# Three edits to a hybrid decoder block: router logits on two halves of the array, fewer idle products, shared squares and a split store at the end

## The chip, the cores and the metric

The kernel runs on one core of one Trainium2 chip. The time is device microseconds of one execution, the median over several; the kernel before took 1893.37 us (three runs, 1891.93 to 1896.53). The engines are PE (TensorE; PEld are its weight loads), DVE (VectorE), ACT (ScalarE), POOL (GpSimd) and SP, whose queue issues nearly all DMA.

## The reference

One decoder layer over 512 tokens of width 2048, in float32: a modulated RMSNorm, a combined input projection, sliding-window attention (16 heads) beside forgetting attention (16 heads), an output projection, and then a hierarchical mixture of experts. The parts that matter here are the router and the end:

```python
x   = x + g_a * (mixed @ w_out[l])
h2  = rmsnorm(x, norm_moe_g[l]) * (1.0 + sc_m) + sh_m

g_logits = (t @ w_group) + b_group            # 4 groups, top 1
e_logits = ((t @ w_expert) + b_expert).reshape(N, N_GROUPS, EXPERTS_PER_GROUP)
e_in = take_along_axis(e_logits, g_sel)       # the 8 experts of that group
top_val, top_idx = lax.top_k(e_in, 2)
...                                           # 2 of 32 SwiGLU experts per token, width 512
x = x + g_m * moe
return rmsnorm(x, final_g)                    # (1, 512, 2048)
```

## The kernel before, in words

The order of the work on every engine is written out by hand: each engine executes its instructions in the order in which the program issues them, and waits on semaphores for its inputs. The 512 tokens are four blocks (tb = 0 to 3) of 128, on the partitions; the width is four chunks (cc) of 512 columns.

**Out-projection and logits.** The output projection runs chunk by chunk (2, 0, 1, 3). For each chunk, products named oq (lines L214 to L216, three for each pair of a high and a low part) accumulate in PSUM; DVE multiplies by the gate and adds to x (gx at L1108, x at L1109). A `Tail` object then takes the chunk's blocks one by one, in steps between the next chunk's products: `tr` transposes x (x1T, copied to x1Ts by ACT at L1127) and squares it, and `logit` forms the chunk's share of the router's 36 logits (4 groups and 32 experts): four products at L1132 with x1Ts as weights and 36 columns of the scaled router weights `wrf` as moving operand. DVE puts the first chunk's share into `lg` (L1134) and adds the next two (L1136). The last chunk's shares stay in one PSUM tile, `lp4`, and are added at L1199, after the row norms `rs` are there. In the same stretch, the modulation vectors of the expert part are formed from w_ada: pieces of 512 KB go through the tile `raw` (which the pieces of w_out share), DVE accumulates half of each (L621), ACT scales the other half (L623) and POOL accumulates it (L624, the first by L619). ACT and DVE also split each piece of w_out into a high and a low part (L175, L176).

**Choosing the experts.** DVE scales the logits by `rs` (L1211), adds the bias (L1212) and runs a row of small steps to the chosen group and experts (`chosen_b`, L1253). PE meanwhile runs 22 products of the identity with itself whose results nobody reads (`turn`, L1229), then the ranking products `rk` (L1257), then 8 more. DVE makes slots and one-hot rows from the ranks (L1468). ACT (L1480) and DVE (L1486) split x times `rs` into two parts, and PE gathers the tokens of each expert with the one-hot rows (xe, L1499); ACT and DVE move the result to SBUF (L1508, L1506).

**Experts.** The 32 experts go in 16 pairs, two experts side by side on the halves of the array (64 columns each): pg and pu (L1363), y (L1385), and the return to token order o (L1407). SP loads the weights, 1 MB a tile, into a ring of tiles, each as soon as the tile's former content has been used (L1309).

**The end.** The last pair's down projection goes in five pieces of columns, `CHUNKS` (three of 512, two of 256): y (L1423), the return to token order (L1442), DVE's addition to x (L1446). After each block of each piece `last_norm` has ACT square the sum and add up the squares (L1605, into `sf5`). After the last, DVE adds up the five sums (L1608), scales them (L1609) and forms the inverse root with ACT's root (L130 to L134); then come eight pieces of 128 by 1024, scaled by DVE (L1616) and stored by SP (L1617). A loop for experts with over 64 tokens follows, which runs no round with these inputs.

Of the kernel before, what the change touches and what calls it, by code (L numbers as in the profile page):

```python
# [8 lines left out]
F32 = mybir.dt.float32  # L9
# [3 lines left out]
AF = mybir.ActivationFunctionType  # L13
OP = mybir.AluOpType
AX = mybir.AxisListType

T = 512
D = 2048
TB = 4
EPS = 1e-6  # L20
# [33 lines left out]
def kernel(  # L54
# [8 lines left out]
    V, S, G, PE, SP = nc.vector, nc.scalar, nc.gpsimd, nc.tensor, nc.sync  # L63
# [8 lines left out]
    def bcast(v, n):  # L72
        return bass.AP(tensor=v.tensor, offset=v.offset, ap=[[0, 128], [1, n]])
# [5 lines left out]
    def flat(t):  # L79
        return t.rearrange("p a b -> p (a b)")  # L80
# [18 lines left out]
    ident = big.tile([128, 128], F32, name="ident")  # L99
# [28 lines left out]
    def rsqrt_(dst, v, tmp):  # L128

        S.activation(tmp, v, AF.Sqrt)  # L130
        V.reciprocal(dst, tmp)
        V.scalar_tensor_tensor(tmp, dst, -0.5, dst, op0=OP.mult, op1=OP.mult)
        V.tensor_mul(tmp, tmp, v)
        V.scalar_tensor_tensor(dst, tmp, 1.5, dst, op0=OP.add, op1=OP.mult)  # L134
# [373 lines left out]
    def bank(shape, name):  # L508

        return pb["pool"].tile(shape, F32, tag=pb["tag"], name=name, bufs=pb["bufs"])  # L510
# [328 lines left out]
    def side_step():  # L839
        f = side_late.pop(0) if side_late else None  # L840
        if f:
            f()

    def attend(segs):


        us = [(u, i) for i, sg in enumerate(segs) for u in sg[0]]
        counts = [sum(1 for _, j in us if j == i) for i in range(len(segs))]
        late, at = None, -1
        for k in range(len(us) + LAG):  # L850
            u, i = us[k] if k < len(us) else (None, len(segs) - 1)
            if i != at:
                if at >= 0:
                    fill.drain()
                at = i
                _, make, total, hook = segs[i]
                fill = make()
                step = total / (2.0 * counts[i] + (2.0 * LAG if i == len(segs) - 1 else 0.0))
                if hook:
                    hook(fill)  # L860
                if u.pre:
                    u.pre()
                    fill.take(1.3)
            if u:
                u.a1()
            if 0 < k <= len(us):
                us[k - 1][0].a2()
            fill.take(step)
            if late:
                late()  # L870
                late = None
            if k >= LAG:
                us[k - LAG][0].b()
                late = us[k - LAG][0].c
            fill.take(step)
            if k + 1 < len(us) and us[k + 1][1] == at and us[k + 1][0].pre:
                us[k + 1][0].pre()
            else:
                side_step()
        late()  # L880
        return fill
# [19 lines left out]
    for g in range(4):  # L901
        VP += natural(256, lambda g=g: accs("accv", f"vb{g}"),
                      lambda tb, o, g=g: S.activation(vbs[g][:, tb, :], o, AF.Copy))

    def fills(i):
        for kind, n, *to in FILLS[i]:
            if kind == "v":
                for v in VP[n:to[0]]:
                    yield from v
            else:  # L910
                yield from (queries2 if kind == "q" else heads2)(n)
# [59 lines left out]
    def out_first():  # L971

        rr = mx["rr"]
        for cc in range(3):
            oacc[cc] = accs4(f"op{cc}")
            for n in range(4):
                hi, lo = ws.get()
                if cc == 2 or n < 3:
                    for j in range(2):
                        k = 2 * n + j  # L980
                        if not cc and k + AH < 8:
                            mixed(k + AH, rr)
                        out_kt(oacc[cc], hi, lo, n, j)
                        if not cc and k in (4 - AH, 7 - AH):
                            load_x1(int(k == 7 - AH))
                        yield 2.6
                else:
                    for tb in range(TB):
                        for j in range(2):
                            out_kt(oacc[cc], hi, lo, n, j, (tb,), last=7)  # L990
                        m = spare()
                        V.tensor_mul(m, oacc[cc][tb], gates[0][:, cc * 512:(cc + 1) * 512])
                        G.tensor_add(x1[cc][:, tb, :], x1[cc][:, tb, :], m)
                        yield 1.3

    wrf = wr.rearrange("p c j e -> p (c j) e")
# [27 lines left out]
    def more_o(fill):  # L1024
# [3 lines left out]
    total = lambda i: 2.56 * sum(to[0] - n if to else 8 for _, n, *to in FILLS[i])  # L1028
    last6 = list(fox_units((6,), qks, vbs))
    f = attend([  # L1030
        (swa_units(((0, 2), (1, 3), (4, 6), (5, 7))[i]) if i < 4 else
         fox_units((i - 4,), qks, vbs) if i < 10 else last6[:LAST], lambda i=i: Fill(fills(i), side, RATE), total(i),
         hooks.get(i))
        for i in range(11)
    ] + [(last6[LAST:] + list(fox_units((7,), qks, vbs)), lambda: Fill(out_first()), LAST_FILL, router)])
# [20 lines left out]
    mo = ctx.enter_context(tc.tile_pool(name="mo", bufs=1, reuse_waits="tile"))  # L1056
    gm = mo.tile([128, D], F32, name="gm")
    ss2 = mo.tile([128, TB, 4], F32, name="ss2")
    lg = mo.tile([128, TB, 36], F32, name="lg")

    def sm(shape, name, dt=F32):
        return mo.tile(shape, dt, name=name)

    def bc(t, shape):
        return t.to_broadcast(shape)

    rs = sm([128, TB], "rs")
    ss3 = sm([128, TB], "ss3")
    iota = sm([128, 128], "iota")
# [21 lines left out]
    class Tail:  # L1091
# [35 lines left out]
            S.activation(self.xT[tb], t, AF.Copy)  # L1127

        def logit(self, tb):
            lp = self.lp4[:, tb, :] if self.last else bank([128, 36], f"lp_{self.cc}_{tb}")  # L1130
            for j in range(4):
                PE.matmul(lp, self.xT[tb][:, j, :], wrf[:, self.cc * 4 + j, :], start=j == 0, stop=j == 3)  # L1132
            if self.cc == 2:
                V.tensor_copy(lg[:, tb, :], lp)  # L1134
            elif not self.last:
                V.tensor_add(lg[:, tb, :], lg[:, tb, :], lp)  # L1136

        def steps(self):
            for tb in range(TB):
# [22 lines left out]
    tail = Tail(2, oacc[2])  # L1162
# [3 lines left out]
    for cc, first in ((0, 4), (1, 4), (3, 0)):  # L1166
        steps = chain(steps, tail.steps())
        ops = []
        for i in range(4):
            k = bank6 % 6  # L1170
# [3 lines left out]
        tail = Tail(cc, ops)  # L1174
# [21 lines left out]
    tail.logit(2)  # L1196
    rms_x1()
    tail.logit(3)
    V.tensor_add(lg, lg, tail.lp4)  # L1199
    pst.close()  # L1200
    frt.close()

# [5 lines left out]
    pb["pool"], pb["tag"], pb["bufs"], hold[0] = ps, "y", 4, True  # L1208
    while side_late:
        side_step()  # L1210
    V.tensor_mul(lg, lg, bc(rs[:, :, None], [128, TB, 36]))  # L1211
    V.tensor_add(lg, lg, bc(brt[:, None, :], [128, TB, 36]))  # L1212

    def one_hot(v, n, mx_, name):
# [11 lines left out]
    def turn(n):  # L1226

        for _ in range(n):
            PE.matmul(idle[:, :128], ident, ident, start=True, stop=True)  # L1229

    turn(22)
    gl = lg[:, :, 0:4]
    gmax = sm([128, TB], "gmax")
    V.tensor_reduce(gmax, gl, axis=AX.X, op=OP.max)
# [20 lines left out]
    for tb in range(TB):  # L1255
        for k in range(tb + 1):
            PE.matmul(rk[:, tb, :], before if k == tb else ones_b, chosen_b[:, k].rearrange("p g e -> p (g e)"),  # L1257
                      start=k == 0, stop=k == tb)
    turn(8)
    place = sm([128, TB, 4, 8], "place")  # L1260
    pf = place.rearrange("p t g e -> p t (g e)")
    V.scalar_tensor_tensor(place, chosen_b, FAR, bc(off.rearrange("p a b e -> p (a b) e")[:, None], [128, TB, 4, 8]),
                           op0=OP.mult, op1=OP.add)
# [19 lines left out]
    HID = cw[:, 5120:5632]  # L1283
# [4 lines left out]
    YT = [cw[:, 5632:6144], more_f[:, 1, :], big.tile([128, 512], F32, tag="wr", name="yt2"), HID]  # L1288
# [6 lines left out]
    def ring_tile():  # L1295

        n = nld[0]
        nld[0] += 1
        if 8 <= n < 12 or 20 <= n < 24:
            return rp_.tile([128, 4, 512], F32, tag=f"x2{n % 12 - 8}", name=f"w{n}")  # L1300
        k = n if n < 8 else n - 4 if n < 20 else n - 8
        return (mo, rp_)[k // 4 % 2].tile([128, 4, 512], F32, tag="w", name=f"w{n}", bufs=4)
# [211 lines left out]
    def total(tb):  # L1514

        if not x2s:
            x2s.extend(rp_.tile([128, D], F32, tag=f"x2{i}", name=f"x2_{i}") for i in range(TB))
        return x2s[tb]
# [77 lines left out]
    sf5 = sm([128, TB, 5], "sf5")  # L1596
    sf, rf, tf = sm([128, TB], "sf"), sm([128, TB], "rf"), sm([128, TB], "tf")

    def last_norm(cols, tb=0):
        if cols is None:  # L1600
            SP.dma_start(fg, bcast(final_g, D))
            return
        c0, c1 = cols
        i = CHUNKS.index(cols)
        S.activation(HID[:, :c1 - c0], total(tb)[:, c0:c1], AF.Square, accum_out=sf5[:, tb, i:i + 1])  # L1605
        if c1 < D or tb < 3:
            return
        V.tensor_reduce(sf, sf5, axis=AX.X, op=OP.add)  # L1608
        V.tensor_scalar(sf, sf, 1.0 / D, EPS, op0=OP.mult, op1=OP.add)  # L1609
        rsqrt_(rf, sf, tf)  # L1610
        for tb in range(TB):
            y = ring_tile()
            for h in range(2):
                sl = slice(h * 1024, (h + 1) * 1024)
                yv = flat(y)[:, sl]
                V.scalar_tensor_tensor(yv, total(tb)[:, sl], rf[:, tb:tb + 1], fg[:, sl], op0=OP.mult, op1=OP.mult)  # L1616
                SP.dma_start(out[tb * 128:(tb + 1) * 128, sl], yv)  # L1617
# [113 lines left out]
```

## Time and profile before

| | |
|---|---|
| median of three runs | 1893.37 us |
| the profiled execution: time, span | 1895.8 us, 1893.9 us |
| mean granted TensorE clock | 0.981 |
| busy: PE, PEld, DVE, ACT, POOL | 96%, 60%, 54%, 40%, 15% |
| DMA | 573.84 MB, 303 GB/s on average |
| the chain that ended last | PE 74%, DMA 8%, ACT 7%, DVE 7%, issue 3%, POOL 1% |
| out-projection with the logits | about 764 to 891 us |
| choosing experts to the first expert product | about 891 to 906 us |
| expert pairs | to about 1866 us |
| squares, root, stores | to 1893.9 us |

A row of the timeline reads: start, duration, engine, line, operation, out<-in, shapes, and in brackets the idle time before it and what ended it. "x8" merges eight instructions. Each float32 product appears as two records. A table by stretches gives busy time of the engines in each stretch, then the granted clock, the share of time in which the DMA engines were busy, and GB/s. The chain lists what each step on the way to the end was released by.

### The profile page before, as it was taken

Reading aid. Unit: us, or ns where it says so; the run is one execution under the profiler, and the core shown is the slowest. Engines: PE = TensorE matmul, PEld = TensorE weight load, DVE = VectorE, ACT = ScalarE, POOL = GpSimd, SP = SyncE. Lnnn points to the kernel's source line nnn. Section 1 sums busy time; section 2 is a strip of 40 time slices with the busy share of each in tenths; the row PEclk is TensorE's granted clock in tenths of the full one; section 3 lists DMA queues with packets and bytes.
Section 4 is the critical chain, followed back from the end, with each engine's and each line's share of the span. In section 5 each row is a group of like instructions: output and inputs, shape, how many; then the busy total and the mean of one; then the engine's idle time right before and its main releaser. Section 6 shows DMA issues by size and latency. Waiting matters only on the chain.

```text
span 1893.9 us, 26581 instructions
## 1 busy us (share of the span) xinstructions
PE 1810.1 (96%) x10045; PEld 1131.1 (60%) x10045; DVE 1018.6 (54%) x1812; ACT 748.7 (40%) x1462; POOL 288.2 (15%) x217
## 2 busy tenths in 40 slices
PE   7998999899899999999999999999999999999995
PEld 5668887787787777778544454444444444444432
DVE  4334676666566545757555454544554545545435
ACT  3235656565555443345523233232322323323213
POOL 0000434443354321445000000000000000000000
PEclk8998999999999999999999999999999999999998
DMA  9984555565566342668989999999999999999995
GB/s 338 352 274 106 169 164 152 165 196 173 160 186 186 113 142 78 208 214 295 369 344 397 420 419 421 421 420 420 420 418 421 416 420 420 419 420 416 420 413 215
DMA packets 208791, 573.84 MB, mean 303 GB/s; under 512 B 22624, under 2 KB 110728, under 8 KB 159888
## 3 DMA queue, kind: packets, MB, share of 16 engines
q1 hardware_dynamic: 207744, 572.00, 80.3%
q8 instruction: 81, 1.33, 0.3%
q14 instruction: 54, 0.44, 0.1%
q10 hardware_dynamic: 912, 0.07, 0.0%
HBM read 567.82 MB, written 4.19 MB: 302 GB/s over the span
## 4 chain that ended last, share of the span: by engine, by line
PE 74%; DMA 8%; ACT 7%; DVE 7%; issue 3%; POOL 1%; SPq 0%; DVEq 0%; ACTq 0%; POOLq 0%
PE pu L1363 12%; PE pg L1363 11%; PE y L1385 9%; PE xe L1499 7%; PE o L1407 5%; DMA w<-in_w_up_dram 4%; PE qp L214 3%; PE qp L216 3%; PE qp L215 3%; DMA raw<-in_w_ada_dram 2%; PE gv L325 2%; PE acc L214 1%; PE acc L215 1%; PE acc L216 1%; PE ob L826 1%
## 5 line engine op out<-in xcount | busy, mean ns | idle before, releaser
L1363 PE MATMUL pu<-w,cw 128*64 128x512 f32 x1024 | 239.3, 593 | 4.7 <-DMA w<-in_w_up_dram 4.7
L1363 PE MATMUL pg<-w,cw 128*64 128x512 f32 x1024 | 235.5, 598 | 1.3 <-ACT cw L1508 0.8
L1508 ACT ACTIVATE cw<-xe,shM,scM 128x128 f32<-128x128 f32 x128 | 58.5, 458 | 429.2 <-PE xe L1499 396.2
L1385 PE MATMUL y<-w,more_f 128*64 128x512 f32 x960 | 214.2, 598 | 4.1 <-ACT xp_whi L1480 2.3
L1506 DVE TENSOR_SCALAR cw<-xe,scM,shM 128x128 f32<-128x128 f32 x128 | 52.4, 410 | 299.3 <-ACT cw L1508 299.3
L624 POOL TENSOR_TENSOR gb<-gb,raw 128x512 f32<-128x512 f32 x112 | 162.1, 1448 | 275.8 <-ACT raw L623 211.4
L1410 DVE SCALAR_TENSOR_TENSOR x<-o,wpair,x 128x512 f32<-128x512 f32 x240 | 163.2, 743 | 19.3 <-PE o L1407 19.3
L1363 PEld LDWEIGHTS pu<-w,cw 128*64 128x64 f32 x1024 | 76.0, 137 | 154.1 <-issue 140.3
L1480 ACT ACTIVATE xp_whi<-x,rs 128x256 fp32r<-128x256 f32 x236 | 162.6, 762 | 0.9 <-DVE rs L134 0.9
L1385 PEld LDWEIGHTS y<-w,more_f 128*64 128x64 f32 x960 | 71.2, 137 | 134.4 <-issue 111.1
L1363 PEld LDWEIGHTS pg<-w,cw 128*64 128x64 f32 x1024 | 69.7, 136 | 133.5 <-issue 128.4
L176 DVE TENSOR_TENSOR wlo_s<-raw,whi_s 128x512 fp32r<-128x512 f32 x96 | 91.4, 953 | 107.7 <-ACT whi_s L175 107.6
L1486 DVE SCALAR_TENSOR_TENSOR xp_wlo<-x,rs,xp_whi 128x256 fp32r<-128x256 f32 x232 | 144.8, 681 | 2.2 <-ACT xp_whi L1480 2.2
L621 DVE SCALAR_TENSOR_TENSOR ga<-raw,csil,ga 128x512 f32<-128x512 f32 x112 | 111.3, 994 | 26.2 <-DMA raw<-in_w_ada_dram 25.6
L1499 PE MATMUL xe<-cr,xp_whi 128*128 128x256 f32 x472 | 120.5, 294 | 0.0
L1499 PEld LDWEIGHTS xe<-cr,xp_whi 128*128 128x128 f32 x472 | 88.7, 188 | 47.3 <-issue 45.4
L1499 PE MATMUL xe<-cr,xp_wlo 128*128 128x256 f32 x472 | 114.3, 281 | 0.0
L214 PE MATMUL qp<-hT_hi,whi_s 128*128 128x512 f32 x256 | 107.3, 419 | 0.0
L216 PE MATMUL qp<-hT_hi,wlo_s 128*128 128x512 f32 x256 | 101.2, 395 | 0.0
L215 PE MATMUL qp<-hT_lo,whi_s 128*128 128x512 f32 x256 | 101.2, 395 | 0.0
L623 ACT ACTIVATE raw<-raw,csil 128x512 f32<-128x512 f32 x112 | 79.8, 713 | 34.0 <-DMA raw<-in_w_ada_dram 32.7
L1499 PEld LDWEIGHTS xe<-cr,xp_wlo 128*128 128x128 f32 x472 | 88.9, 188 | 0.0
(445 smaller groups left out, 3372.5 us busy)
## 6 DMA issues: line engine op xcount, KB each, us to landing
w<-in_w_gate_dram SPq DMA_DIRECT2D x128, 1024.0 KB, 10.6
w<-in_w_up_dram SPq DMA_DIRECT2D x128, 1024.0 KB, 13.9
w<-in_w_down_dram SPq DMA_DIRECT2D x126, 1024.0 KB, 10.3
raw<-in_w_ada_dram SPq DMA_DIRECT2D x128, 512.0 KB, 4.2
raws<-in_w_ada_dram SPq DMA_DIRECT2D x64, 512.0 KB, 8.9
raw<-in_w_in_dram SPq DMA_DIRECT2D x160, 128.0 KB, 2.8
raw<-in_w_out_dram SPq DMA_DIRECT2D x32, 512.0 KB, 3.8
raw<-in_w_in_dram SPq DMA_DIRECT2D x48, 256.0 KB, 3.3
```

What stands on the lines that cost most here:

```text
L214: PE.matmul(o, lhi, rhi, start=first, stop=False, **kw)
L215: PE.matmul(o, lhi, rlo, start=False, stop=False, **kw)
L216: PE.matmul(o, llo, rhi, start=False, stop=last, **kw)
L621: V.scalar_tensor_tensor(a, ts[n][:, j, :], s, a, op0=OP.mult, op1=OP.add)
L624: G.tensor_add(a, a, ts[n][:, j, :])
L1363: PE.matmul(o[64 * e:64 * e + 64, :], self.xe(cc)[:, j, 64 * e:64 * e + 64], w[cc, e][:, j, :], start=cc == 0 and j == 0, stop=cc == 3 and ...
L1385: PE.matmul(ys[dc][64 * e:64 * e + 64, :], HT[:, k, 64 * e:64 * e + 64], self.wd[k, e][:, dc, :], start=k == 0, stop=k == 3)
L1407: PE.matmul(o, self.ohT[:, tb, :], v, start=i == 0, stop=i == 1)
L1410: V.scalar_tensor_tensor(x2, o, self.w_col(tb), x2 if self.n else x1[dc][:, tb, :], op0=OP.mult, op1=OP.add)
L1480: S.activation(hi[tb], xv, AF.Identity, scale=s)
L1486: V.scalar_tensor_tensor(lo[tb], xv, s, hi[tb].bitcast(F32), op0=OP.mult, op1=OP.subtract)
L1499: PE.matmul(t[:, j, :], v[tb][:, j, :], OHS[:, tb].rearrange("p q s -> p (q s)"), start=tb + i == 0, stop=tb + i == TB)
```

## The change

Three edits, joined.

*Logits.* For chunks 2, 0 and 1 the roles of the operands are exchanged: the 36 columns of `wrf` are the weights and the transposed x is the moving operand, 128 columns. The four products of a visit go alternately to output partitions 0 to 35 and 64 to 99, that is to two halves of the array's columns. DVE then copies or adds both parts into a new tile `lgT` (partitions by tokens). In the last chunk a product of `lgT` with `both`, two identities stacked at partitions 0 and 64, turns the sum back and adds the halves up in `lp4`, ahead of the four products of the old form. The addition of `lp4` goes: one instruction multiplies `lp4` by `rs` straight into `lg`. POOL clears and fills the two new tiles.

*Idle products.* 15 instead of 22, and 6 instead of 8.

*End.* For blocks 2 and 3 of the last piece, DVE squares instead of ACT. POOL adds up the first four pieces' sums and scales them; DVE adds the fifth in one instruction. The last block's store is in pieces of 1024, 640 and 384 columns instead of two of 1024.

```diff
--- before.py
+++ after.py
@@ -1058,6 +1058,13 @@
     ss2 = mo.tile([128, TB, 4], F32, name="ss2")
     lg = mo.tile([128, TB, 36], F32, name="lg")
 
+    lgT = mo.tile([128, T], F32, name="lgT")
+    G.memset(lgT, 0.0)
+    both = mo.tile([128, 36], F32, name="both")
+    G.memset(both, 0.0)
+    for e in (0, 64):
+        G.tensor_copy(both[e:e + 36, :], ident[e:e + 36, e:e + 36])
+
     def sm(shape, name, dt=F32):
         return mo.tile(shape, dt, name=name)
 
@@ -1127,13 +1134,23 @@
             S.activation(self.xT[tb], t, AF.Copy)
 
         def logit(self, tb):
-            lp = self.lp4[:, tb, :] if self.last else bank([128, 36], f"lp_{self.cc}_{tb}")
+            sl = slice(tb * 128, (tb + 1) * 128)
+            if self.last:
+                lp = self.lp4[:, tb, :]
+                PE.matmul(lp, lgT[:, sl], both, start=True, stop=False)
+                for j in range(4):
+                    PE.matmul(lp, self.xT[tb][:, j, :], wrf[:, self.cc * 4 + j, :], start=False, stop=j == 3)
+                return
+            lp = bank([128, 128], f"lp_{self.cc}_{tb}")
             for j in range(4):
-                PE.matmul(lp, self.xT[tb][:, j, :], wrf[:, self.cc * 4 + j, :], start=j == 0, stop=j == 3)
-            if self.cc == 2:
-                V.tensor_copy(lg[:, tb, :], lp)
-            elif not self.last:
-                V.tensor_add(lg[:, tb, :], lg[:, tb, :], lp)
+                e = 64 * (j % 2)
+                PE.matmul(lp[e:e + 36, :], wrf[:, self.cc * 4 + j, :], self.xT[tb][:, j, :], start=j < 2, stop=j > 1)
+            for e in (0, 64):
+                o = lgT[e:e + 36, sl]
+                if self.cc == 2:
+                    V.tensor_copy(o, lp[e:e + 36, :])
+                else:
+                    V.tensor_add(o, o, lp[e:e + 36, :])
 
         def steps(self):
             for tb in range(TB):
@@ -1196,7 +1213,7 @@
     tail.logit(2)
     rms_x1()
     tail.logit(3)
-    V.tensor_add(lg, lg, tail.lp4)
+    V.tensor_mul(lg, tail.lp4, bc(rs[:, :, None], [128, TB, 36]))
     pst.close()
     frt.close()
 
@@ -1208,7 +1225,6 @@
     pb["pool"], pb["tag"], pb["bufs"], hold[0] = ps, "y", 4, True
     while side_late:
         side_step()
-    V.tensor_mul(lg, lg, bc(rs[:, :, None], [128, TB, 36]))
     V.tensor_add(lg, lg, bc(brt[:, None, :], [128, TB, 36]))
 
     def one_hot(v, n, mx_, name):
@@ -1228,7 +1244,7 @@
         for _ in range(n):
             PE.matmul(idle[:, :128], ident, ident, start=True, stop=True)
 
-    turn(22)
+    turn(15)
     gl = lg[:, :, 0:4]
     gmax = sm([128, TB], "gmax")
     V.tensor_reduce(gmax, gl, axis=AX.X, op=OP.max)
@@ -1256,7 +1272,7 @@
         for k in range(tb + 1):
             PE.matmul(rk[:, tb, :], before if k == tb else ones_b, chosen_b[:, k].rearrange("p g e -> p (g e)"),
                       start=k == 0, stop=k == tb)
-    turn(8)
+    turn(6)
     place = sm([128, TB, 4, 8], "place")
     pf = place.rearrange("p t g e -> p t (g e)")
     V.scalar_tensor_tensor(place, chosen_b, FAR, bc(off.rearrange("p a b e -> p (a b) e")[:, None], [128, TB, 4, 8]),
@@ -1602,16 +1618,25 @@
             return
         c0, c1 = cols
         i = CHUNKS.index(cols)
-        S.activation(HID[:, :c1 - c0], total(tb)[:, c0:c1], AF.Square, accum_out=sf5[:, tb, i:i + 1])
+        v = total(tb)[:, c0:c1]
+        if c1 == D and tb > 1:
+            V.tensor_tensor_reduce(YT[1][:, :c1 - c0], v, v, scale=1.0,
+                                   scalar=0.0, op0=OP.mult, op1=OP.add, accum_out=sf5[:, tb, i:i + 1])
+        else:
+            S.activation(HID[:, :c1 - c0], v, AF.Square, accum_out=sf5[:, tb, i:i + 1])
+        if i == 3 and tb == 3:
+
+            for k in range(1, 4):
+                G.tensor_add(sf, sf5[:, :, 0] if k == 1 else sf, sf5[:, :, k])
+            G.tensor_scalar(sf, sf, 1.0 / D, EPS, op0=OP.mult, op1=OP.add)
         if c1 < D or tb < 3:
             return
-        V.tensor_reduce(sf, sf5, axis=AX.X, op=OP.add)
-        V.tensor_scalar(sf, sf, 1.0 / D, EPS, op0=OP.mult, op1=OP.add)
+        V.scalar_tensor_tensor(sf, sf5[:, :, 4], 1.0 / D, sf, op0=OP.mult, op1=OP.add)
         rsqrt_(rf, sf, tf)
         for tb in range(TB):
             y = ring_tile()
-            for h in range(2):
-                sl = slice(h * 1024, (h + 1) * 1024)
+            for c0, c1 in ((0, 1024), (1024, 2048)) if tb < 3 else ((0, 1024), (1024, 1664), (1664, 2048)):
+                sl = slice(c0, c1)
                 yv = flat(y)[:, sl]
                 V.scalar_tensor_tensor(yv, total(tb)[:, sl], rf[:, tb:tb + 1], fg[:, sl], op0=OP.mult, op1=OP.mult)
                 SP.dma_start(out[tb * 128:(tb + 1) * 128, sl], yv)
```

## The prediction

> **What bounds the kernel now.** I read the chain that ended last, then the expert part in a table by stretches and the waits of SP's DMA queue, then the chain again for the out-projection alone.
>
> ```profile
> span 1893.9 us, 26581 instructions
> ...
> 1229.70 3.43 PE pu L1363 x16
> ...
> 1676.01 13.89 DMA w<-in_w_up_dram
> ...
> 1850.40 3.65 PE y L1423 x14
> ...
> 960.00:980.00 20.00, 20.00 (x104) 8.95 (x102) 12.25 (x20) 7.75 (x13) 0.00 (x0) 1.00 0.79 319
> ...
> 1020.00:1040.00 20.00, 20.00 (x101) 8.61 (x102) 10.26 (x18) 8.05 (x14) 0.00 (x0) 1.00 1.01 419
> ...
> SPq L1309 <- PE pg L1363: 93.6, 14, 15.7
> ```
>
> The columns of the two stretches are length, busy time of PE, PEld, DVE, ACT and POOL with counts, clock, DMA share, GB/s. From 1020 us on the DMA engines are full (1.01, 419 GB/s), and the chain has one long wait for weights per two pairs of experts (13.89 us at 1676) until the last weights have landed at 1850.40. Before that, DMA is not full (0.79 at 960): there SP waits until PE has used a weight tile (93.6 us on L1363). So three places can move the end. What starts the expert chain earlier frees tiles earlier, and the full stretch with its fixed bytes starts and ends earlier by the same amount. PE work saved after that is worth nothing. And the 43.5 us from 1850.40 to the span's end at 1893.9 run one after the other.
>
> The out-projection, where all sixteen logit visits fall (four chunks of 512 columns by four token blocks), has a chain of its own:
>
> ```profile
> by line: DMA raw<-in_w_ada_dram 26.6%; issue 9.4%; DVE lo_s L176 6.2%; POOL gb L624 6.0%; PE oq L215 4.6%; DVE gx L1108 4.5%; PE oq L216 4.3%; PE oq L214 4.1%; DVE x L1109 4.1%; ACT raw L623 3.2%; ACT hi_s L175 2.8%; PE lp L1132 2.5%; ACT x
> ...
> 834.44 0.81 PE lp L1132 x8
> ...
> 872.82 0.81 PE lp L1132 x8
> ...
> 877.71 1.08 PE lp L1132 x8
> ...
> 884.39 0.82 PE lp L1132 x8
> ...
> 840.00:860.00 20.00, 19.50 (x99) 16.05 (x98) 9.88 (x12) 9.51 (x16) 13.12 (x9) 1.00 0.75 248
> ```
>
> Its largest share is the wait for w_ada pieces (26.6%), which go round five buffers; the logits (L1132) hold 2.5%, in four visits. PE is busy 19.50 of 20 us in the last row, but that counts modelled ends; the chain passes mostly elsewhere.
>
> **The change part by part: logits on two halves.** Before, a block's logits are four products with x1T as weights and 36 moving columns. They become four with 36 columns of weights and 128 moving ones, alternating between two halves of the array, and two additions on DVE instead of one.
>
> ```profile
> 872.66 0.97 PE L1132 MATMUL lp<-wr,x1Ts 128*128 128x36 f32 x8
> ...
> 873.47 0.48 PE L214 MATMUL oq<-hi_s,mx_hi 128*128 128x512 f32 x1
> ...
> 874.46 0.18 DVE L1136 TENSOR_TENSOR lg<-lg,lp 128x36 f32<-128x36 f32 x1
> ...
> 888.17 0.69 DVE L1114 CUSTOM_DVE_ANT_0 gx<-x 128x512 f32<-128x512 f32 x1
> ...
> 888.84 1.98 PE L1132 MATMUL lp<-wr,x1Ts 128*128 128x36 f32 x16
> 889.09 0.60 ACT L1127 ACTIVATE x1Ts<-x1T 128x512 f32<-128x512 f32 x1 [0.63 <-issue]
> ...
> 890.86 0.30 DVE L1199 TENSOR_TENSOR lg<-lg,lp 128x144 f32<-128x144 f32 x1 [0.28 <-PE lp L1132]
> ...
> 904.08 0.28 PE L1499 MATMUL xe<-cr 128*128 128x256 f32 x1
> 904.29 1.08 PE L1363 MATMUL pg<-w,cw 128*64 128x512 f32 x4
> ...
> 906.19 2.79 PE L1363 MATMUL pg<-w,cw 128*64 128x512 f32 x12 [0.82 <-ACT cw L1508]
> ...
> 908.91 0.38 PE L1499 MATMUL xe<-cr,more_r 128*128 128x256 f32 x1
> ...
> POOL gb L619 <- DMA raw<-in_w_ada_dram: 51.5, 1, 51.5
> ...
> L1484 POOL TENSOR_TENSOR xp_wlo<-cw,xp_whi 128x256 fp32r<-128x256 f32 x4 | 3.0, 747 | 11.0 <-ACT cw L1483 11.0
> ```
>
> A visit now lasts from 872.66 to the next product at 873.47: 0.81 us, eight records (two for each product), 0.10 each. Half-array products already run here: 16 records of 512 columns take 3.43 us (1229.70), 0.214 each; a quarter of the columns gives 0.054, eight of them 0.43. To that comes the change of layout. Going from whole to half array, the last xe at 904.08 is followed after 0.21 by pg, where a record of that run takes 0.12: 0.09 lost. Back, twelve pg records from 906.19 end at 908.77 at 0.214 each and xe starts at 908.91: 0.14 lost. A visit should take 0.43+0.23=0.66, a gain of 0.15. Twelve visits save 1.8 us of PE; three of the four on the chain (834, 872, 877) are of this kind: **−0.45 us**. Ends: 0 if none counts, −4.6 if all twelve count with no loss on the way (12×0.38).
>
> [...]
>
> On DVE one instruction of 0.18 becomes two. No row has 36 partitions by 128 from PSUM; between 36 columns (0.18) and 144 (0.30) a straight line gives 0.28, so +0.38 a visit, 4.6 us in all. DVE is busy 9.88 of 20 us in the row above; in the chain its long stretches there are lo_s and the gx/x pairs. I take 0 on the path; ends 0 and +4.6. Behind the second addition in DVE's queue stand L621, which frees raw buffers, and L176, on which PE waits.
>
> The last chunk keeps the old form and gains one product per block (lgT against two stacked identities): two records, 0.20 us. Block 0's lies on the chain (884.39): **+0.20**. Block 1's is not on the chain. Those of blocks 2 and 3 lengthen the 1.98 us at 888.84, but its second half waited for the copy at 889.09 (0.60, to 889.69); the end moves from 890.82 to about 891.07, +0.25. Behind it DVE now runs three instructions over 144 columns (add, scale by rs, add bias), 0.30 plus gaps, 0.34 each; one goes: −0.34. Together **−0.08**. From there on DVE has no idle time up to L1486's end, so this passes on.
>
> The added set-up (memsets of lgT and both, two copies) is on POOL about 720 us; POOL then waits for data for 51.5 us, which hides them; without that cover they would delay POOL's share of w_ada by under 4 us, at 0.75 for each with 256 columns or less (L1484) and twice that for the 512 of lgT.
>
> **Idle products.**
>
> ```profile
> 892.46 5.07 PE L1229 MATMUL idle<-ident 128*128 128x128 f32 x44
> ...
> 897.56 0.29 DVE L1253 TENSOR_TENSOR chosen_b<-gsel,oh 128x128 bf16<-128x128 f32 x1
> ...
> 898.17 2.03 PE L1229 MATMUL idle<-ident 128*128 128x128 f32 x16
> ...
> 899.34 1.30 DVE L1468 TENSOR_TENSOR cr<-iota,slot 128x512 fp32r<-128x512 f32 x2
> ...
> 900.55 2.43 DVE L1486 SCALAR_TENSOR_TENSOR cr<-x,rs,mr 128x256 fp32r<-128x256 f32 x4
> ...
> 946.59:950.00 3.41, 1.10 (x8) 0.62 (x8) 2.62 (x16) 0.91 (x3) 0.00 (x0) 1.00 1.00 420
> 950.00:953.41 3.41, 3.41 (x10) 0.97 (x8) 0.58 (x4) 0.00 (x0) 0.00 (x0) 0.50 1.01 425
> ```
>
> The 22 run to 897.53 and the ranking product starts at 897.91 when DVE has chosen; with 15 (0.113 per record, 14 fewer) they end about 896.1 and PE waits 1.7 us. The 8 end at 900.2 just as the first one-hot halves (L1468) are there; with 6 PE is ready 0.45 earlier and waits for DVE at 900.0. DVE is then the limit (L1486 from 900.55, two runs of 2.4 us, to about 905.3), and PE waits for the gathered columns until 906.19. Gain 0, −0.1 at most. The clock is the risk: the last two rows, 3.41 us each, show PE busy 1.10 us and then half clock throughout the next. A gap of 1.7 us leaves 1.7 busy if it falls whole into such a stretch, not far from it. Half clock over the gathers would cost up to 1.7 us, less the 0.82 that PE waits at 906.19: +0.9; I take 0.
>
> [...]
>
> **The end.**
>
> ```profile
> 1869.24 3.22 DVE L1446 SCALAR_TENSOR_TENSOR x<-o,wpair,x 128x256 f32<-128x256 f32 x8
> ...
> 1872.29 0.42 ACT L1605 ACTIVATE cw<-x 128x256 f32<-128x256 f32 x1
> ...
> 1874.45 0.17 DVE L1608 TENSOR_REDUCE sf<-sf 128x4 f32<-128x20 f32 x1 [2.00 <-ACT cw L1605]
> ...
> 1874.86 0.20 ACT L130 ACTIVATE tf<-sf 128x4 f32<-128x4 f32 x1 [0.44 <-DVE sf L1609]
> ...
> 1875.90 9.65 DVE L1616 SCALAR_TENSOR_TENSOR w<-x,rf,cw 128x1024 f32<-128x1024 f32 x8
> ...
> out_dram<-w SPq DMA_DIRECT2D x8, 512.0 KB, 3.1
> ...
> 1880.00:1882.00 2.00, 0.00 (x0) 0.00 (x0) 2.00 (x3) 0.00 (x0) 0.00 (x0) 0.50 1.02 410
> ```
>
> ACT squares the last chunk in four steps of 0.54 from 1872.29 until DVE goes on at 1874.45, while DVE has finished its additions at 1872.46 and waits 2.0 us. The change moves two squares to DVE. ACT's two then end at 1873.37. DVE: three additions of 0.40 from 1870.85 to 1872.06, square, addition, square. The square of 512 columns at 888.17 keeps DVE 0.82 until its next instruction; at 256, less 0.27, 0.55. So 1872.61, 1873.01, 1873.56. POOL, which has nothing else to do there, sums chunks 0 to 3 meanwhile: its last two small instructions start after ACT's at 1872.26, and even at the 0.75 of 128x256 (L1484) they end at 1873.76; I take 0.25 each, 1872.8, since they have four columns. One DVE instruction replaces the reduction and the scaling, so the root starts at 1873.79 instead of 1874.86: **−1.07**. Ends: −0.3 (POOL slow, or the squares' writes to sf5 wait for POOL's reads of that tile) and −1.2.
>
> The last block's store becomes 1024, 640 and 384 columns. DVE does nine instructions for eight; 256 columns take 0.40 and 1024 take 1.21, so a fixed 0.13: **+0.10**. The last transfer is 0.375 of its size. Its 3.1 us to landing do not grow over eight transfers, so no queue stands ahead of it; 512 KB at some 410 GB/s last 1.28, and 0.62 of that is 0.8 at best. But DVE makes 512 KB in 1.21, about as fast, so the 640 piece is still moving. Ends 0 and −0.8; I take **−0.3**, nearer to the bandwidth row. SP issues once more, off the path.
>
> **Sum:** −0.45+0.20−0.08 in the middle, −1.07+0.10−0.30 at the end: −1.6 us. The profiled execution took 1895.8 (span 1893.9, 1.9 around it), 2.4 above the median; I apply the difference to the median: 1893.37−1.6=**1891.8**.
>
> **Rivals.** *PE sets the pace of the out-projection.* Then twelve visits count at 0.38: −4.6, with the end −1.3: 1887.5. For it: 19.50 busy of 20; against it: the chain's 26.6% on DMA and the losses at 904 and 908.
>
> *The second addition on DVE decides.* It holds back L621 and so the buffers' return; all twelve at 0.38 give +4.6, less the end's 1.3 and the 0.3 of the middle: 1896.4, slower. For it: lo_s, gx and x on DVE hold 14.8% of the stage's chain; against it: DVE is half idle. From 1.6 us on the path, four visits of twelve, the whole gain is gone.
>
> *The end's new sums do not do what they should:* POOL or sf5 holds DVE up, −0.3 there and nothing from the store: with the middle's 0.3, 1892.8.
>
> *Half clock after the shorter idle run:* +0.9, 1892.7.
>
> **How the numbers follow.** Forecast 0.50 (1889.8 to 1893.2), PE rival 0.10, DVE rival 0.17, end 0.15, clock 0.08. About 0.3%, 5.7 us, is what a measurement of this kernel can tell from no change. Only the PE rival reaches it downwards: faster 0.10; of the DVE rival a third, were L621's delay to be paid again at each turn of the buffers, is over it: slower 0.05; same 0.85. The range must take the two far rivals in part and the spread of the three times before (1891.9 to 1896.5): 1888.5 to 1896.0.
>
> **What would show it.** A visit of 0.66 between its first product and the next whole-array product; w_ada still leading the out-projection's chain; the first pg run after the choice at about 906; pairs of additions of 0.28 on lgT; DVE's wait before the root gone, the root 4.5 us after the first 256-wide addition (5.6 before); the last landing under 3.1. Wrong would prove me: the expert chain starting over 2 us earlier or later, or the clock at 0.50 about 899 to 903.

## The result and the profile after

The changed kernel takes 1884.12 us (median of five runs, 1880.14 to 1885.75), the kernel before 1893.19 us beside it (five runs, 1891.93 to 1896.53): ratio 0.9943, 95% interval 0.9924 to 0.9961. That is 9 us, where 1.6 were forecast, and below the range, which began at 1888.5. The profiled execution took 1880.14 us, 4.0 below its median; that of before took 1895.8, 2.6 above. The two traces therefore lie 6.6 us further apart than the medians, and a difference between them is trusted below only where other runs repeat it.

The chain that ended last, of the changed kernel (start, duration, what):

```profile
span 1878.5 us, 26586 instructions
...
1307.17 12.41 DMA w<-in_w_up_dram
...
1426.78 11.96 DMA w<-in_w_up_dram
...
1664.73 12.19 DMA w<-in_w_up_dram
...
1831.94 7.25 PE y L1439 x32
```

Before, seven waits for weights stood in this chain from 1100 us on, the last before the last piece's y at 1850.40. Here three are left, and that y runs at 1831.94 without one. One long stretch of the expert part as a whole, before and then after (length, busy time of PE, PEld, DVE, ACT, POOL with counts, clock, DMA share, GB/s):

```profile
1100.00:1800.00 700.00, 693.44 (x3456) 326.56 (x3454) 351.47 (x585) 207.72 (x347) 0.00 (x0) 1.00 1.01 419
```

```profile
1100.00:1800.00 700.00, 696.81 (x3477) 326.40 (x3476) 354.98 (x589) 208.15 (x347) 0.00 (x0) 1.00 1.01 424
```

The DMA engines are full in both (1.01). But the same full engines move 424 GB/s instead of 419, in a stretch whose instructions the change does not touch. The full stretch of before, from 1020 to 1835 us, at 424 instead of 419 is 815×(1−419/424) = 9.6 us shorter, give or take 2 us, since the rates are rounded. That is the size of the gain; what the rate hangs on, the experiments must show.

### The profile page after: what moved, and what is told of

Same layout as the page of the kernel before. It is cut to its first block, busy times and chain, and to the rows that moved or that the text cites. A ratio compares the mean times of both kernels' runs of the same rounds, so it can differ in the third digit from the quotient of the medians.

```text
span 1878.5 us, 26586 instructions
## 1 busy us (share of the span) xinstructions
PE 1798.1 (96%) x10035; PEld 1117.7 (60%) x10035; DVE 1023.4 (54%) x1827; ACT 748.2 (40%) x1458; POOL 289.7 (15%) x225
## 4 chain that ended last, share of the span: by engine, by line
PE 75%; DVE 8%; ACT 6%; DMA 5%; issue 3%; POOL 1%; SPq 0%; DVEq 0%; ACTq 0%; POOLq 0%
PE pu L1379 12%; PE pg L1379 12%; PE y L1401 10%; PE xe L1515 7%; PE o L1423 5%; PE qp L214 2%; PE qp L216 2%; PE qp L215 2%; DMA raw<-in_w_ada_dram 2%; DMA w<-in_w_up_dram 2%; PE gv L325 2%; PE acc L214 1%; DVE lo_s L176 1%; PE acc L215 1%; PE acc L216 1%
## 5 line engine op out<-in xcount | busy, mean ns | idle before, releaser
L621 DVE SCALAR_TENSOR_TENSOR ga<-raw,csil,ga 128x512 f32<-128x512 f32 x112 | 106.9, 954 | 20.7 <-DMA raw<-in_w_ada_dram 19.9
## 6 DMA issues: line engine op xcount, KB each, us to landing
raw<-in_w_in_dram SPq DMA_DIRECT2D x160, 128.0 KB, 2.7
```

What stands on the lines that cost most here:

```text
L621: V.scalar_tensor_tensor(a, ts[n][:, j, :], s, a, op0=OP.mult, op1=OP.add)
```

## Theories, and experiments on the place of the ring

What the change alters for these transfers is where they go. The tiles of a partition are laid out one behind the other, and `lgT` (2048 bytes) and `both` (144, taken as 160) are allocated ahead of the weight ring's four places in the pool `mo`. These began 128096 bytes into a partition, 96 past a multiple of 256, and now begin at 130304, a multiple of 256. The ring's other four places (pool `wring`, where half of the loads go) stayed at 163808, 224 past one.

Theory *place*: a transfer whose rows begin at a multiple of 256 bytes is faster. Rival *early start*: the edits let the expert chain begin earlier (first product of the experts at 898.5 us instead of 904.3 in the traces), and the rest follows.

**Unused tiles in the kernel before.** The instructions on the path stay; 160, 128 or 32 bytes are put ahead of `mo`'s ring.

```
+    pad = mo.tile([128, 40], F32, name="pad")     # 160 bytes; 32 elements or 8 in the others
+    G.memset(pad, 0.0)
```

> The kernel before with nothing of the change: only an unused tile of 160 bytes per partition ahead of the weight ring's four tiles in the pool mo, so that these start at offset 128256, a multiple of 256, instead of 128096 (32 past a multiple of 64). Theory place: the expert stretch's rate rises from 420 to 424 GB/s or more as in the changed kernel, and the time falls by about 6 us, to 1887 or 0.997 of before. Rival, early start (the changed kernel gains because its expert chain starts earlier, and the rate of 424 is a drift): no change, 1893, rate 420.

> As the kernel with 160 bytes, with 128 bytes: the four ring tiles move by as much but start at 128224, again 32 past a multiple of 64. Theory place, if the 64-byte step is what counts: no change, 1893 and 420 GB/s. If only the move itself or the memory's other contents count: like the run with 160 bytes. Rival early start: no change.

> As before with 32 bytes: the ring tiles start at 128128, a multiple of 64 (and 128) but not of 256. Theory place with a step of 64: 1887 and 424 GB/s as with 160 bytes; with a step of 256: 1893 and 420. Rival early start: 1893.

**The changed kernel, its ring put back.** The same with 96 bytes in the changed kernel: `mo`'s ring is 96 past a multiple of 256 again.

> The changed kernel with an unused tile of 96 bytes ahead of the ring, which then starts at 130400, 32 past a multiple of 64 (96 past one of 256, as before). Theory place: the rate falls back to 420 GB/s and the time to about 1890; what is left to before, some 3 us, is the out-projection, the choice and the end. Rival early start: 1884 as the changed kernel.

**The other half of the ring.** An unused tile of 224 bytes ahead of the pool `wring` brings its places to 163584, a multiple of 256: in the kernel before alone, there together with the 160 bytes, and in the changed kernel (where five small tiles of `weights()` share an old one to make room).

```
+    pr_ = ctx.enter_context(tc.tile_pool(name="rpad", bufs=1, side="right"))
+    padr = pr_.tile([128, 56], F32, name="padr")
+    G.memset(padr, 0.0)
     rp_ = ctx.enter_context(tc.tile_pool(name="wring", ...
```

> The kernel before with wring's four places at multiples of 256 and mo's four where they were (96 past one): the other half of the ring alone. Theory place, with each half worth the same until TensorE sets the pace: as the 160-byte pad (mo's half alone, 1885.0), 1884 to 1886 us and 423 GB/s. Rival (the gain belongs to mo's half, or to where its places lie against each other): 1891 to 1894 us, 419 to 420 GB/s.

> The kernel before, with unused tiles alone (160 bytes in mo, 224 bytes on the right side), so that all eight places of the ring begin at multiples of 256: no instruction of the path is another. Theory place: twice the step of the 160-byte pad alone (1885.0), so 1893.5 - 18 = 1875 to 1877 us, and a descriptor's median time from issue to landing lower for all three kinds of weights. Rival: no more than the 160-byte pad gave, 1883 to 1886 us.

> The changed kernel, with a 224-byte pad on the right side of SBUF so that the ring's other four places (wring, 163808 = 224 past a multiple of 256) begin at 163584, a multiple of 256; five small tiles of weights() are put into the old r1 tile to make room. Nothing else. Theory place (each transfer whose destination begins off a multiple of 256 bytes is slower): half of the ring's loads go to wring, half to mo, and mo's half gave about 9 us, so this gives about as much again: 1884.1 - 9 = 1875 us (1871 to 1879), and 428 to 430 GB/s between 1100 and 1800 us of the span. Rival (only mo's half was worth anything, or TensorE is now the bound): 1882 to 1885 us and 424 GB/s.

What was measured, by the bytes past a multiple of 256 (GB/s from 1100 to 1800 us of each profile; ratios against the kernel before on the same chip):

| code | `mo` / `wring` | us | ratio, 95% interval | GB/s |
|---|---|---|---|---|
| before | 96 / 224 | 1893.19 | | 419 |
| before, pad 32 | 128 / 224 | 1894.29 | 1.0004, 0.9994 to 1.0013 | 420 |
| before, pad 128 | 224 / 224 | 1897.31 | 1.0014, 1.0005 to 1.0023 | 418 |
| before, pad 160 | 0 / 224 | 1884.98 | 0.9949, 0.9935 to 0.9962 | 423 |
| before, wring | 96 / 0 | 1885.06 | 0.9955, 0.9942 to 0.9969 | 425 |
| before, both | 0 / 0 | 1881.41 | 0.9943, 0.9927 to 0.9959 | 425 |
| changed, pad 96 | 96 / 224 | 1893.02 | 0.9991, 0.9981 to 1.0000 | 419 |
| changed | 0 / 224 | 1884.12 | 0.9943, 0.9924 to 0.9961 | 424 |
| changed, both | 0 / 0 | 1880.07 | 0.9924, 0.9911 to 0.9937 | 426 |

An unused tile of 160 bytes does to the kernel before what the whole change did. With 128 or 32 bytes in its place the gain is gone, though 128 past a multiple of 256 is still a multiple of 128; and of the three starts that gain (128256, 130304, 163584) none is a multiple of 512. So the step is at 256. The changed kernel without the place is back at the old time, where 1890 was expected: the place is nearly the whole gain. Either half of the ring by itself gives 8 to 9 us.

The traces show it in the experts' stage alone, whenever that begins. From the first product pg to the last the profiles need 933.4 to 938.5 us with no half of the ring in place, 924.3 to 928.8 with one, 922.7 to 926.3 with both. The changed kernel with the 96 bytes starts its experts at 899.9 us, 4.4 earlier than before, and still needs 937.4. *Place* is shown, and *early start* falls: how early the experts begin differs by several us between profiles, in part from work ahead of the out-projection, and does not by itself carry to the end.

Places off a multiple of 256 may not be wholly alike: with both halves 224 past one, the time is 1.0014 of before, with an interval that leaves out 1. Fewer than 96 bytes past were not tried.

The second half gave less than expected on top of the first (3.6 and 4.1 us by the medians, not 9, and 425 to 426 GB/s, not 428 to 430); 1881.41 and 1880.07 lie between the theory's times and the rival's. This is the same stretch with the whole ring in place, in the changed kernel:

```profile
1100.00:1800.00 700.00, 697.89 (x3495) 329.68 (x3494) 355.73 (x590) 208.89 (x349) 0.00 (x0) 1.00 1.01 426
```

PE is busy 697.89 of 700 us, where it was 693.44, and in the chain of this kernel no long step is a wait for weights any more. What DMA could still give is therefore hidden behind PE.

With half of the ring in place the rate is 424 GB/s for 419, 1.2% more. With the whole ring in place the queue's lines for the same 700 us (packets, MB, share of 16 engines' span), before and then in the changed kernel, are:

```profile
q1 hardware_dynamic: 40247, 293.07, 100.9%
```

```profile
q1 hardware_dynamic: 40823, 297.30, 100.8%
```

That is 1.4% more packets in the same busy time. Why a place at a multiple of 256 is the faster one was not shown.

**Shorter rows.** If the place costs something at each row, an assumption of the author's, it should cost more there. At the start, rows are near 1 KB: 28.11 MB in 26811 packets. The hardware queue's line in the stretch from 40 to 120 us, before and then in the kernel described next:

```profile
q1 hardware_dynamic: 26811, 28.11, 108.9%
```

```profile
q1 hardware_dynamic: 29697, 30.59, 107.8%
```

This kernel is the changed one with all places that receive weights at multiples of 256: the ring, `raws` and `raw`. It only shares, moves and pads small tiles.

> The changed kernel with every place that takes weights at a multiple of 256: ring, raws (160 and 128 past one before) and raw (224 past one); a few small tiles share a place, and unused tiles make up the rest. The first 120 us move 350 GB/s in rows of 1 and 2 KB, shorter than the ring's 8 KB. [...] Rival (TensorE or something other than the place sets the first 120 us): 1879 to 1881 us, and 350 GB/s there.

From 40 to 120 us, before and then in this kernel (columns as above):

```profile
40.00:120.00 80.00, 80.00 (x621) 52.51 (x621) 29.45 (x59) 21.91 (x41) 0.00 (x0) 1.00 1.09 353
```

```profile
40.00:120.00 80.00, 80.00 (x622) 52.56 (x621) 30.03 (x59) 22.05 (x42) 0.00 (x0) 1.00 1.08 384
```

384 GB/s for 353 at nearly the same DMA share: 9% for rows of 1 KB, where half of the rows of 8 KB gave 1.2%. A packet took 1.089×16×80 us/26811 = 52.0 ns and now takes 46.5, 11% less. The author's estimate for the time, 4 to 13 us below the 1880.07 of the ring alone, rested on a cost for each row whose size no run shows, and failed: 1878.51 us (1878.04 to 1882.07, ratio 0.9921, 0.9907 to 0.9934), 1.6 below, with overlapping runs. The row says why: PE is busy all 80 us with either rate, and the faster transfers only finish earlier. It is the fastest version found, and not told apart from the changed kernel with the ring alone in place.

## Experiments on the edits themselves

With the places equal, the edits are left. Three pairs have equal places: 1893.02 against 1894.08 of before (ratio 0.9991), 1884.12 against 1884.98, 1880.07 against 1881.41. The change is worth 0.9 to 1.3 us by these medians; by the means of the same runs it is 1.7 (interval 0 to 3.6, by the ratio), 1.6 and 3.2, the last with one run of the kernel before at 1888.39. The prediction's sum was 1.6. Which edit gives it:

**Logits alone**, end and idle products as before, the whole ring in place.

> Only the logits on two halves, all ring places at multiples of 256, idle products and end as before. Prediction's terms: visits -0.45, last chunk about +0.1: 0.3 us below the kernel before so placed (1881.4), 1881.1. By the stage marks (first product of x1 turned to first product of the experts, 130.1 on average without the change and 128.8 with it) 1.3 us below: 1880.1. The end accounts for the rest against 1880.1 of the whole change so placed: -1.0 or 0.

1881.84 us (1880.12 to 1883.44), against 1881.41 (1880.49 to 1888.39) without the edit: nothing that can be measured, and too coarse to choose between 0.3 and 1.3. What is left, 1.8 us to 1880.07, would belong to the end or to the idle products, but these runs overlap too.

**22 and 8 idle products**, the rest changed, the whole ring in place.

```
-    turn(15)
+    turn(22)
...
-    turn(6)
+    turn(8)
```

> The changed kernel with all eight ring places at multiples of 256, and 22 and 8 idle products again instead of 15 and 6. By the prediction's term (0) 1880.1 us as with 15 and 6, and full clock in the whole choice, where three of five profiles of the changed kernel show 0.92 in a sixth of it. Rival (fewer idle products let the clock drop, 0.9 us or more each time): 1878 to 1879.5 us.

1880.25 us (1878.79 to 1882.49) against 1880.07: no difference, as predicted.

**Two halves for the last store**, in the changed kernel, and in the one with the whole ring in place.

```
-            for c0, c1 in ((0, 1024), (1024, 2048)) if tb < 3 else ((0, 1024), (1024, 1664), (1664, 2048)):
+            for c0, c1 in ((0, 1024), (1024, 2048)):
```

> The changed kernel with the last store in two halves of 1024 columns again (the split 1024, 640, 384 undone). By the prediction's term (-0.3 for the smaller last transfer, +0.1 for the ninth operation) this is 0.2 us slower; by the stage marks of the traces (store scaling to end 18.0 before, 18.6 to 18.8 changed) it is 0.6 us faster. In time 1883.5 to 1884.3; the marks of the profile tell more than the time.

> Both: the changed kernel with all ring places at multiples of 256 and the last store in two halves. Theory place: as the run with all places aligned, and 0 to 0.6 us less: 1874 to 1875 us. Rival: 1882 to 1885 us.

1881.44 us (1880.72 to 1885.92) and 1880.25 us (1878.43 to 1884.01): neither is told apart from its split version (1884.12 and 1880.07); the first came out below what was expected, and the second between its two expectations. From the first scaling to the span's end it is 18.7 and 18.4 us with halves, 18.6 and 18.7 split: the split does nothing that shows in the traces either. The suspicion that it costs 0.6 us falls; what that was stands with the end below.

## Why the prediction was wrong, step by step

**The step that failed** is the first part's "the full stretch with its fixed bytes starts and ends earlier by the same amount". It takes the rate for fixed, and so for the change part by part a new tile had no cost but POOL's work to clear it ("the added set-up"). The tiles' bytes were in the diff, the ring lay behind them in the same pool, and the full DMA engines, which the prediction named as the bound, were the one place where a shift could count. There was no term for it in the sum and no rival. All the miss, 7.7 us, and a little more lies there: 160 unused bytes, with none of the edits present, raised the rate from 419 to 423 GB/s and took 9 us off the time.

**The bound** was read rightly: most of the gain could only come from weights that land earlier, and they did. The PE rival's time (1887.5) is on the side where the result fell, but not by its mechanism. The sign named for being wrong, experts that start over 2 us earlier, came true in this pair of traces (898.5 for 904.3), but it is no measure of the gain: 3.4 of the 5.8 us were there at the first product of the out-projection, and the profile of the changed kernel with the whole ring in place and the last store in halves starts its experts at 905.0, later than before.

**Logits.** The out-projection's chain, changed kernel:

```profile
800.07 0.30 DVE lgT L1151
...
855.75 0.26 DVE lgT L1153
...
867.12 0.56 PE lp L1147 x8
...
878.61 0.89 PE lp L1142 x8
...
885.44 3.49 PE gr L596 x4
888.93 3.35 PE idle L1245 x30
```

A visit takes 0.56 us; the prediction had 0.66 from 0.43 and two changes of layout of 0.23 together. If 0.43 is right, these lose about 0.13. The size of that loss, taken from two other rows, was too large; that there is one rests on the estimate of 0.43 alone. The gain is 0.25 a visit, not 0.15. In the last chunk a block takes 1.04 us (0.15 more stands ahead of the 0.89) for 0.82 before: +0.22, where +0.20 was predicted. On DVE a copy (L1151) and an addition (L1153) show as single steps of 0.30 and 0.26 on the chain, where 0.28 was taken and nothing put on the path. From the first transposition of x1 to the first product of the experts the seven profiles with this edit (those of the version with all places at 256 aside) need 127.4 to 130.2 us, mean 129.1; six without it 129.7 to 130.6, mean 130.2. The predicted 0.33 lies inside that scatter, and so does 2 us; the time of the logits alone does not decide it.

**Idle products.** 0 was right in time. The clock did fall near this place in some profiles of the changed kernel. Here is the stretch of 10 us ahead of the ranking, with a clock of 0.83, in which `gr` above takes 3.49:

```profile
880.00:890.00 10.00, 9.91 (x59) 7.60 (x58) 6.95 (x24) 6.95 (x13) 2.28 (x3) 0.83 0.81 299
```

The 3.4 us ahead of the fall, with transpositions and products of 36 columns on PE:

```profile
881.90:885.30 3.40, 3.31 (x31) 3.23 (x30) 2.05 (x8) 1.88 (x6) 0.00 (x0) 1.00 0.83 320
```

It fell to 0.50 at 885.3 us, before the first of the 15 idle products at 888.93, so their number cannot have caused it, and this profile's way to the experts, 128.0 us, is the second shortest of the seven. The predicted +0.9 of that rival is not seen. What made the clock fall is open: PE was busy 3.31 of 3.40 us ahead of it, so the prediction's reading, that a fall follows a stretch with PE idle for much of it, does not cover this one. Of seven profiles with the new logits four show a clock of 0.92 in one stretch of 21 to 22 us between 861 and 901 us; three, and five without them, show 1.00 in these stretches. Whether the logits bring it was not tried.

**The end.** The timeline of the changed kernel's last piece:

```profile
1854.37 2.82 DVE L1462 SCALAR_TENSOR_TENSOR x<-o,wpair,x 128x256 f32<-128x256 f32 x7
...
1857.23 0.42 DVE L1623 CUSTOM_DVE_ANT_0 more_f<-x 128x256 f32<-128x256 f32 x1
...
1857.83 0.20 POOL L1631 TENSOR_SCALAR sf<-sf 128x4 f32<-128x4 f32 x1
...
1858.09 0.43 DVE L1623 CUSTOM_DVE_ANT_0 more_f<-x 128x256 f32<-128x256 f32 x1
...
1858.86 0.20 ACT L130 ACTIVATE tf<-sf 128x4 f32<-128x4 f32 x1 [0.39 <-DVE sf L1634]
...
1859.90 9.79 DVE L1641 SCALAR_TENSOR_TENSOR w<-x,rf,cw 128x1024 f32<-128x1024 f32 x9
```

The root starts 4.49 us after the first addition (1858.86−1854.37; predicted 4.5, before 5.6), with POOL done (1858.03) ahead of DVE's second square. This step was right: −1.1. From the last piece's first y to the first scaling, seven profiles with the changed end need 28.0 to 28.9 us, seven with the old one 29.1 to 30.3; at equal places of the ring that is 1.1 to 1.3 less.

The stores were not right. The lines of the store in the changed kernel, and then in the kernel with the logits alone, which has the old end (minimum, median and maximum of the issue in ns, and of the way to landing in us):

```profile
L1642 SPq DMA_DIRECT2D out_dram<-w x9: 332/333/918, 1861.2 to 1869.7; - x9
...
DMA to landing us min/median/max: 3.4/3.4/4.1
```

```profile
L1636 SPq DMA_DIRECT2D out_dram<-w x8: 332/332/361, 1862.4 to 1870.8; - x8
...
DMA to landing us min/median/max: 2.6/2.7/2.7
```

The last landing takes 4.1, not under 3.1. But the traces hold landings of the first two stores alone, and, where the store is split, of the last one. So the prediction's 3.1, and its reading that it does not grow over eight transfers, came from the first two stores and not from the last; that is one more step that failed. What can be compared for the last store is its last packet: it ends 3.65 us after the last issue before and 3.76 in the changed kernel, so the smaller piece is done no sooner.

Nor is the rest due to the pieces: in all the profiles with the new end one issue takes 0.60 to 1.07 us and the median of the recorded landings is 3.3 to 4.0, with halves too; in all with the old end no issue is over 0.40 and that median is 2.6 to 3.1. From the first scaling to the span's end seven profiles each need 18.6 us on average with the new end and 18.0 with the old; with the ring's half in `mo` in place, 18.5 (six) and 17.8 (three). So in place of the predicted −0.2 for scaling and store stands +0.6 to +0.7, out of the 1.1 won before it. Which part of the new end (the sums on POOL, the squares on DVE) delays the stores is open: it wasn't tried.

**The sum** of the steps, −1.6, against 0.9 to 3.2 measured at equal places, is right within what the runs tell, but in part by luck: with the stores at +0.6 and three visits at 0.25 it would be −1.1, and the runs cannot tell the two apart. Its agreement does not bear out its terms.

## What to carry to other kernels

Where DMA is full, look at where each buffer begins before the arithmetic of an edit: in this kernel it was worth 9 us whether half of the weights' places began at a multiple of 256 bytes, and any tile allocated ahead of a buffer moves it. When a new kernel differs in a stretch that its edit does not touch, compare the rate there first, and test it with an unused tile in the old kernel. Here the gain ended where the next engine was full, at 698 of 700 us of PE.

## What the runs showed of the hardware that was not expected

Full DMA engines are not one rate: with a DMA share of 1.01 they moved 418 to 420 GB/s into places off a multiple of 256 bytes, whether 96, 128 or 224 past it, and 423 to 425 with half of the places on it, and 425 to 426, then with PE busy 697.3 to 697.9 of 700 us, with all of the ring's places on it. With rows of about 1 KB the step was from 352 to 384 GB/s.
